# Block sums of the down projection's weights, made in DRAM by accumulating transfers

## The chip, the cores and the metric

The kernel runs on one core of one Trainium2 chip. The metric is the device time of one execution in microseconds (us), of which the runs give a median. The engines are TensorE (PE, with its weight loads as PEld), VectorE (DVE), ScalarE (ACT), GpSimd (POOL) and SyncE (SP, which here only issues transfers). Each runs its own list of instructions in order. Transfers (DMA) are done by 16 DMA engines that all the queues share.

## The reference

Two layers of an encoder over one sequence of 512 tokens and 1024 features. Each layer has a token mixer and a gated feed-forward part; the change touches the last product of the latter.

```python
def mixer_sublayer(x, w_in, pool_w, ...):
    proj = x @ w_in
    ...
    y = bidirectional_ssd(xh, dt_raw, a_log, dt_bias, bm, cm, d_skip)
    ...
    return merged @ w_out

def conv_ffn(x, w_up, ffn_conv_w, ffn_conv_b, w_down):
    h = dwconv_centred(x @ w_up, ffn_conv_w, ffn_conv_b)
    gate, val = jnp.split(h, 2, axis=-1)
    return (jax.nn.gelu(gate, approximate=False) * val) @ w_down

def reference(...):
    for i in range(DEPTH):                       # DEPTH = 2
        x = layer_norm(ALPHA * x + mixer_sublayer(x, ...), ...)
        x = layer_norm(ALPHA * x + conv_ffn(x, ...), ...)
    return x
```

`w_down` of a layer has 2816 rows and 1024 columns.

## The kernel before

**Products.** Every large product is done in fp32 by halves: a tile is split into a rounded high part and the rest, and `mm3` (L381 to L383) makes three matmuls of each product. The weights go through `WeightStream` (L38 to L109): SP issues the load of 1 MB into `wraw` (L66, two buffers), ACT copies the high part `wh` (L90), DVE subtracts it for `wl` (L91), two steps ahead of PE's use.

**Order.** PE's order is the order in which the code is written. On the other engines a scheduler places the instructions by its own estimate of times, within what the data and the buffers allow.

**Mixer.** The state-space mixer of a layer works in eight units `unit(u)` of four heads, two units to a group; they run as background jobs beside the input projection's matmuls. In a unit, ACT's queue brings rows of cumulated decays to all partitions (`m<-acd`), POOL masks them (`affine_select` on `m`, L994), POOL weights the inputs (`xw`, L1051), PE makes states of them (`stp`, L1068), POOL folds the states (`s`, L1076) and adds up the outputs (`y`, L1057 and L1109).

**Down projection.** `strassen_projection` (from L597) does `r @ w_down` with r the gated hidden values, transposed, by Winograd's form of Strassen's scheme. The 22 blocks of 128 rows of `w_down` make 11 pairs; of a pair, b00 and b01 are the left and right half of the even block, b10 and b11 of the odd one. There are seven half-sized products, gathered in the banks v, y, z and x. They want four blocks as they are and four sums of blocks: t1 = b01 - b00, t3 = b11 - b01, t2 = t3 + b00 (up to sign as the code has them) and t4 = b10 - t2. Before the change POOL makes the sums in SBUF as the weights arrive:

```python
g.tensor_tensor(raw[:, 1536:2048], raw[:, 1024:1536], raw[:, 512:1024], op=ALU.subtract)  # L137
g.tensor_tensor(raw[:, 512:1024], raw[:, 512:1024], raw[:, 0:512], op=ALU.subtract)       # L138
self.make_t2(i, raw)            # L126: one more subtraction, into xths or xtls
```

and in the second half `lower` makes t4 (L154). `xths` and `xtls` (L607) are the space of tiles that are free in this stage. For each pair SP loads 512 KB + 256 KB in the first half. The halves of r that don't fit stay in DRAM (`asp`, written by POOL's queue, L1368) and are fetched again by SP (`fetch`, L619; 384 KB per pair), and split by ACT and DVE (`cut`, L621 to L626).

Of the kernel before, what the change touches and what calls it, by code (L numbers as in the profile page):

```python
# [38 lines left out]
class WeightStream:  # L39
# [3 lines left out]
    def __init__(self, nc, tc, pool, plan, ahead, raw_bufs, bufs):  # L43
        self.nc, self.tc, self.pool = nc, tc, pool
        self.plan = plan
        self.subs = [(i, j) for i, r in enumerate(plan) for j in r["order"]]
        self.ahead = ahead
        self.raw_bufs, self.bufs = raw_bufs, bufs
        self.raw = {}
        self.done = {}  # L50
        self.next_raw = 0
        self.next_sub = 0
        self.pos = 0
        self.seq = []
        self.extra = {}
# [4 lines left out]
    def _load(self, i):  # L60
        r = self.plan[i]
        raw = self.pool.tile([P, 2048], F32, tag="wraw", name=f"wraw{i}", bufs=self.raw_bufs)
# [14 lines left out]
    def _split(self, s):  # L77
        i, view = self.seq[s]
        self.load(i + 1)
        src = view(self.raw[i])  # L80
        _, a, b = src.shape
        if s in self.extra:
            pool, bufs = self.extra[s]
        else:
            pool, bufs = self.pool, self.bufs
        h = pool.tile([P, 1024], F32R, tag="wh", name=f"wh{s}", bufs=bufs)
        l = pool.tile([P, 1024], F32R, tag="wl", name=f"wl{s}", bufs=bufs)
# [19 lines left out]
class StrassenWeights:  # L107
# [4 lines left out]
    def __init__(self, nc, tc, pairs):  # L112
        self.nc, self.tc, self.pairs = nc, tc, pairs
        self.t2 = {}
        self.raw0 = None

    def open(self, tiles):

        for t in tiles:
            for i in range(t.shape[1]):  # L120
                self.t2[len(self.t2)] = (t, i)
        self.make_t2(0, self.raw0)

    def make_t2(self, i, raw):
        t, j = self.t2[i]
        self.nc.gpsimd.tensor_tensor(  # L126
            t[:, j, :], raw[:, 1024:1536], raw[:, 512:1024], op=ALU.subtract
        )

    def direct(self, raw):  # L130

        return raw.rearrange("p (a b) -> p a b", a=2)[:, :, 0:512]

    def sums(self, i, raw):

        g = self.nc.gpsimd
        g.tensor_tensor(raw[:, 1536:2048], raw[:, 1024:1536], raw[:, 512:1024], op=ALU.subtract)  # L137
        g.tensor_tensor(raw[:, 512:1024], raw[:, 512:1024], raw[:, 0:512], op=ALU.subtract)  # L138
        if i:
            self.make_t2(i, raw)  # L140
        else:
            self.raw0 = raw
        return raw.rearrange("p (a b) -> p a b", a=2)[:, :, 512:1024]

    def two(self, q):
        t, j = self.t2[2 * q]
        return t[:, j : j + min(2, self.pairs - 2 * q), :]

    def lower(self, q, o, raw):

        t = self.two(q)
        n = t.shape[1]
        b = raw[:, o : o + n * 512].rearrange("p (a b) -> p a b", a=n)
        self.nc.gpsimd.tensor_tensor(t, b, t, op=ALU.subtract)  # L154
        return b

    def plan(self, w, first):

        raws, direct, sums = [], [], []
        for i in range(self.pairs):  # L160
            a, b = 2 * i * P, (2 * i + 1) * P
            raws.append({"srcs": [w[a : a + P, :].unsqueeze(1),
                                  w[b : b + P, 512:1024].unsqueeze(1)], "order": range(2)})
            direct.append((first + i, self.direct))
            sums.append((first + i, partial(self.sums, i)))
        seq = []
        for i in range(self.pairs - 2):
            seq += [direct[i], sums[i]]
        seq += direct[-2:] + sums[-2:]
        odd = w.rearrange("(k two p) c -> two p k c", two=2, p=P)[1, :, :, 0:512]  # L170
        lower, t2, t4 = [], [], []
        for i in range(0, self.pairs, 4):
            n = min(4, self.pairs - i)
            r = first + len(raws)
            raws.append({"srcs": [odd[:, i : i + n, :]], "order": range(n)})
            for k in range(0, n, 2):
                q = (i + k) // 2
                lower.append((r, partial(self.lower, q, k * 512)))
                t2.append((r if q else r - 1, lambda raw, q=q: self.two(q)))
                t4.append((r, lambda raw, q=q: self.two(q)))  # L180
        nq = len(t2)
        for q in range(nq - 2):
            seq += [t2[q], lower[q]]
        return raws, seq + t2[-2:] + lower[-2:] + t4
# [40 lines left out]
def weight_plan(l, w_in, pool_w, w_ssd_proj, w_out, w_up, w_down, down):  # L225
# [71 lines left out]
    r, s = down.plan(w_down[l], len(raws))  # L297
# [4 lines left out]
def tile_hybrid_pool_ssd_convffn_encoder(  # L302
# [60 lines left out]
    downs = [StrassenWeights(nc, tc, KF // 2) for _ in range(NL)]  # L363
# [134 lines left out]
    class Norm:  # L498
# [28 lines left out]
        def add(self, c, c0, ps, first=False, last=False):  # L527
# [3 lines left out]
            if first:  # L531
                nc.vector.scalar_tensor_tensor(xs, xs, ALPHA, ps, op0=ALU.mult, op1=ALU.add)
            else:
                nc.vector.tensor_tensor(xs, xs, ps, op=ALU.add)
# [69 lines left out]
    def strassen_projection(l, name, sw, tags, pool, spill, norm):  # L604
# [7 lines left out]
        sw.open([scratch[0], scratch[1][:, : n - KD, :]])  # L612
        again = scratch[1][:, 3:6, :].rearrange("p a b -> p (a b)").rearrange(
            "p (s a b) -> p s a b", s=2, a=3)
# [3 lines left out]
        def fetch(i):  # L618
            nc.sync.dma_start(again[:, i % 2], spill[i])  # L619

        def cut(i):  # L621
            h = pool.tile([P, 4, 256], F32R, tag=f"ah{i}", name=f"{name}h{i}")
            lo = pool.tile([P, 4, 256], F32R, tag=f"al{i}", name=f"{name}l{i}")
            nc.scalar.copy(h[:, :3], again[:, i % 2])
            nc.vector.tensor_tensor(lo[:, :3], again[:, i % 2], h[:, :3], op=ALU.subtract)
# [20 lines left out]
        for i in range(n - 2):  # L646
# [11 lines left out]
            fetch(i)  # L658
# [14 lines left out]
        for i in (n - 2, n - 1):  # L673
            both(yb, (tags[i], 1), s[i - n + 2], 0, False, i == n - 1)
            both(zb, (tags[i], 2), s[i - n + 2], 1, False, i == n - 1)
            fetch(i)
# [4 lines left out]
        for cc in range(2):  # L681
            norm.add(2 + cc, 512, zb[cc])
            norm.add(2 + cc, 0, zb[cc], True)
# [6 lines left out]
        for q in range(nq - 2):  # L690
# [5 lines left out]
            if q == 0:  # L696
                cut(n - 1)
        t2 = [ws.get(), ws.get()]
# [3 lines left out]
        with tc.high_priority():  # L702
            for cc in range(2):
                norm.add(cc, 512, xb[cc])
                norm.add(2 + cc, 512, xb[cc])
# [62 lines left out]
    for l in range(NL):  # L768
# [483 lines left out]
        for g in range(4):  # L1252
# [16 lines left out]
            ujobs.append(unit(2 * g))  # L1269
            ujobs.append(unit(2 * g + 1))  # L1270
# [70 lines left out]
        for j in range(KF):  # L1341
# [83 lines left out]
```

## Time and profile before

| | before |
|---|---|
| median of 3 runs | 1989.69 us (1988.59 to 1989.8) |
| the profiled execution | 1992.83 us, its span 1991.0 us |
| mean granted TensorE clock | 0.993 |
| PE busy | 1931.9 us, 97% |
| DVE / ACT / POOL busy | 68% / 50% / 31% |
| moved by DMA | 232.19 MB, mean 117 GB/s |

The profile is of one execution, 3.1 us above the median. The span is the time from the first to the last instruction seen. Busy shares are means over the whole; a row of windows gives the same for one stretch. In the rows, `out<-in` are the program's names, and a bracket such as [1.63 <-DVE wl L91] says how long the engine had been idle ahead of the instruction and what ended it.

### The profile page before, as it was taken

The numbers are of one execution on the slowest core, as the hardware profiler recorded it, in microseconds if no ns is written. First come the engines' busy times: TensorE is split into PE (matmuls) and PEld (weight loads), VectorE is DVE, ScalarE is ACT, GpSimd is POOL, SyncE is SP. The second block draws the span as 40 slices with busy tenths as digits, with TensorE's granted clock in tenths as the row PEclk, the third lists the DMA queues.
The fourth block names the chain that finished last, engine by engine and source line by source line (L and its number), as shares of the span: only waits on it lengthen the run. The fifth ranks groups of instructions, "written<-read, shape, count | busy, mean of one in ns | idle before, by whom it ended". The sixth has DMA issues, their size and how long they took to land.

```text
span 1991.0 us, 27368 instructions
## 1 busy us (share of the span) xinstructions
PE 1931.9 (97%) x10449; PEld 1616.0 (81%) x10449; DVE 1348.4 (68%) x1945; ACT 998.4 (50%) x1665; POOL 609.0 (31%) x578
## 2 busy tenths in 40 slices
PE   8999999999999999998999999999999999999997
PEld 7878798988888888876788878989888888888765
DVE  5668576775556656679985685667656566666898
ACT  4767666644333444444457776656443334444443
POOL 1244424241111111168303343242411111111773
PEclk9999999999999999999999999999999999999999
DMA  5444434233241334345225344343332414333541
GB/s 159 123 119 117 127 93 140 86 113 115 76 164 49 121 112 134 106 153 190 83 90 160 106 112 124 110 124 105 85 111 92 168 43 130 121 101 116 180 154 51
DMA packets 174691, 232.19 MB, mean 117 GB/s; under 512 B 7872, under 2 KB 128868, under 8 KB 174560
## 3 DMA queue, kind: packets, MB, share of 16 engines
q1 hardware_dynamic: 152144, 178.80, 28.3%
q10 hardware_dynamic: 17712, 34.08, 7.0%
q0 software_dynamic: 4704, 17.56, 2.5%
q8 instruction: 83, 1.36, 0.3%
q14 instruction: 48, 0.39, 0.1%
HBM read 217.31 MB, written 13.11 MB: 116 GB/s over the span
## 4 chain that ended last, share of the span: by engine, by line
PE 78%; DVE 6%; issue 6%; POOL 4%; DMA 3%; ACT 3%; SPq 0%; POOLq 0%; ACTq 0%; DVEq 0%
PE fg L382 7%; PE fg L381 7%; PE fg L383 7%; PE spp L381 3%; PE zp L381 3%; PE spp L382 3%; PE spp L383 3%; PE zp L382 3%; PE zp L383 3%; PE xp L381 3%; DVE wl L91 3%; PE xp L383 3%; PE xp L382 3%; PE stp L1068 2%; PE ydp L1019 2%
## 5 line engine op out<-in xcount | busy, mean ns | idle before, releaser
L91 DVE TENSOR_TENSOR wl<-wraw,wh 128x1024 fp32r<-128x1024 f32 (+1 forms) x330 | 454.1, 1377 | 251.6 <-ACT wh L90 250.0
L90 ACT CAST wh<-wraw 128x1024 fp32r<-128x1024 f32 (+1 forms) x330 | 341.2, 1035 | 503.6 <-PE fg L382 158.0
L383 PE MATMUL fg<-xthm,wl 128*128 128x512 f32 x640 | 249.0, 389 | 0.0
L381 PE MATMUL fg<-xthm,wh 128*128 128x512 f32 x640 | 249.0, 389 | 0.0
L382 PE MATMUL fg<-xtlm,wh 128*128 128x512 f32 x640 | 249.0, 389 | 0.0
L1001 ACT ACTIVATE m<-m,nac 128x128 f32<-128x128 f32 x512 | 159.6, 392 | 52.2 <-POOL m L994 51.7
L994 POOL TENSOR_SCALAR_AFFINE_SELECT m<-m 128x512 f32<-128x512 f32 x128 | 95.0, 765 | 183.5 <-DMA m<-acd 162.9
L381 PEld LDWEIGHTS fg<-xthm,wh 128*128 128x128 f32 x640 | 120.1, 188 | 25.0
L383 PEld LDWEIGHTS fg<-xthm,wl 128*128 128x128 f32 x640 | 120.1, 188 | 24.9
L382 PEld LDWEIGHTS fg<-xtlm,wh 128*128 128x128 f32 x640 | 120.1, 188 | 24.9
L1109 POOL TENSOR_TENSOR y<-y,yo 128x256 f32<-128x256 f32 x96 | 85.4, 898 | 101.6 <-DVE yo L1101 98.8
L381 PE MATMUL spp<-yth,wh 128*128 128x512 f32 x256 | 110.3, 431 | 0.5 <-ACT yth L1149 0.5
L382 PE MATMUL spp<-ytl,wh 128*128 128x512 f32 x256 | 101.2, 395 | 0.7 <-DVE ytl L1150 0.7
L383 PE MATMUL spp<-yth,wl 128*128 128x512 f32 x256 | 101.1, 395 | 0.0
L479 DVE SCALAR_TENSOR_TENSOR xc<-xp,pcwc,xc 128x510 f32<-128x510 f32 (+1 forms) x128 | 95.2, 745 | 7.2 <-ACT xc L473 5.7
L1002 DVE TENSOR_TENSOR m<-m 128x512 f32<-128x512 f32 x64 | 46.7, 730 | 64.8 <-ACT m L1001 55.5
L1051 POOL TENSOR_TENSOR xw<-xtok,wst 128x768 f32<-128x768 f32 x32 | 51.3, 1621 | 121.9 <-ACT xtok L943 99.0
L1363 POOL TENSOR_TENSOR r<-cvv,cg 128x512 f32<-128x512 f32 x22 | 28.4, 1292 | 175.1 <-issue 130.4
L381 PE MATMUL zp<-wh,xthf 128*128 128x256 f32 x256 | 77.6, 303 | 0.0
L1286 POOL TENSOR_TENSOR g<-g,acc 128x512 f32<-128x512 f32 x16 | 27.5, 1720 | 162.3 <-ACT g L1247 150.3
L381 PE MATMUL zp<-wh,xthi 128*128 128x256 f32 x256 | 77.1, 301 | 0.0
L382 PE MATMUL zp<-wl,xthf 128*128 128x256 f32 x256 | 73.0, 285 | 0.0
(403 smaller groups left out, 5214.0 us busy)
## 6 DMA issues: line engine op xcount, KB each, us to landing
wraw<-in_w_in_dram SPq DMA_DIRECT2D x56, 1024.0 KB, 5.5
wraw<-in_w_up_dram SPq DMA_DIRECT2D x44, 1024.0 KB, 5.2
m<-acd ACTq DMA_DIRECT2D x64, 512.0 KB, 4.9
wraw<-in_w_ssd_proj_dram SPq DMA_DIRECT2D x16, 1024.0 KB, 5.1
wraw<-in_w_down_dram SPq DMA_DIRECT2D x22, 512.0 KB, 3.6
asp<-r POOLq DMA_DIRECT2D x22, 384.0 KB, 2.9
xtls<-asp SPq DMA_DIRECT2D x22, 384.0 KB, 3.8
wraw<-in_w_in_dram SPq DMA_DIRECT2D x16, 512.0 KB, 5.3
```

The source lines that it names most:

```text
L90: self.nc.scalar.copy(hv, src)
L91: self.nc.vector.tensor_tensor(lv, src, hv, op=ALU.subtract)
L381: mm(lhsT=ah, rhs=bh, start=first, stop=False)
L382: mm(lhsT=ah, rhs=bl, start=False, stop=False)
L383: mm(lhsT=al, rhs=bh, start=False, stop=last)
L479: nc.vector.scalar_tensor_tensor(dst[:, o0:o1], ps[:, o0 + s : o1 + s], tap, dst[:, o0:o1], op0=ALU.mult, op1=ALU.add,)
L994: nc.gpsimd.affine_select(out=mv, in_=mv, pattern=[[0, NCH], [1 - 2 * d, P]], compare_op=ALU.is_ge, fill=NEG, base=0, channel_multiplier=2 ...
L1001: nc.scalar.activation(mc, mc, AF.Exp, bias=nac[:, c, col : col + 1])
L1002: nc.vector.tensor_tensor(m[:, 0], m[:, 0], m[:, 1], op=ALU.add)
L1019: nc.tensor.matmul(ps[q * 64 : (q + 1) * 64, c * 64 : (c + 1) * 64], lhsT=m[:, 0, t0 : t0 + 64], rhs=xtok[:, c, hh * 64 : (hh + 1) * 64], ...
L1051: nc.gpsimd.tensor_tensor(h4(xw[:, d]), h4(xtok[:, d : d + 3, :]), hb(wst, d, d + 3, d), op=ALU.mult)
L1109: nc.gpsimd.tensor_tensor(y[:, c, :], y[:, c, :], yo[:, d, :], op=ALU.add)
```

## The change

The sums are no longer made by POOL in SBUF. Each layer has three new tensors in DRAM, `t13` (t1 and t3 side by side), `t2` and `t4`, and eight transfers make them from `w_down`, issued on POOL's queue: four copies, and then four transfers with `accum_op=ALU.add`, which add the source to what stands in the destination. One is issued after each `unit(u)`. Every one moves 11 x 128 x 512 values, 2.88 MB, in 1408 rows of 2 KB. Since all of them add, t1, t3, t2 and t4 are plain sums here, and the signs move to the other operand (`q[:, 1]`, `q[:, 3]`) and to three of the final additions (`norm.add(..., op=ALU.subtract)`).

In the down projection the loads of a pair are now 256 KB + 256 KB of `w_down` and 512 KB of `t13`, later `t2`, `b10` and `t4`. The space of `xths` holds two more raw buffers (`raw_at`) in the first half and two split tiles (`cut_at`) in the second; that of `xtls` holds five buffers for the fetched r in place of two, fetched three pairs ahead.

```diff
@@ WeightStream._load, _split
+        if i in self.raw_at:
+            raw = self.raw_at[i]
...
+        if s in self.cut_at:
+            h, l = self.cut_at[s]
@@ StrassenWeights
-    def make_t2(self, i, raw):
-    def sums(self, i, raw):
-    def lower(self, q, o, raw):
...
+    def __init__(self, nc, dram, l, w, pairs):
+        self.nc, self.pairs = nc, pairs
+        self.t13 = dram.tile([P, pairs, 2, 512], F32, name=f"t13_{l}")
+        self.t2 = dram.tile([P, pairs, 512], F32, name=f"t2_{l}")
+        self.t4 = dram.tile([P, pairs, 512], F32, name=f"t4_{l}")
+        self.blocks = w.rearrange("(k two p) (h c) -> two h p k c", two=2, h=2, p=P)
+        b, t1, t3 = self.blocks, self.t13[:, :, 0, :], self.t13[:, :, 1, :]
+        self.steps = [
+            (t1, b[0, 1]), (t3, b[0, 1]), (self.t2, b[1, 1]), (self.t4, b[1, 0]),
+            (t1, b[0, 0], ALU.add), (t3, b[1, 1], ALU.add),
+            (self.t2, t1, ALU.add), (self.t4, self.t2, ALU.add),
+        ]
+
+    def prepare(self, step):
+        dst, src, *op = self.steps[step]
+        if op:
+            self.nc.gpsimd.dma_start(dst, src, accum_op=op[0], max_dma_last_dim=2048)
+        else:
+            self.nc.gpsimd.dma_start(dst, src)
@@ StrassenWeights.plan
+        for i in range(n):
+            raws.append({"srcs": [b[0, 0, :, i : i + 1, :], b[1, 1, :, i : i + 1, :],
+                                  self.t13[:, i, :, :]], "order": range(2)})
@@ strassen_projection
-            nc.sync.dma_start(again[:, i % 2], spill[i])
+            nc.sync.dma_start(again[:, i % 5], spill[i])
...
-            fetch(i)
+            for j in range(i + 3 if i else 0, min(i + 4, n)):
+                fetch(j)
@@ the mixer's loop over groups
-            ujobs.append(unit(2 * g))
-            ujobs.append(unit(2 * g + 1))
+            for u in (2 * g, 2 * g + 1):
+                ujobs.append(unit(u))
+                downs[l].prepare(u)
@@ the gated hidden values
-            nc.vector.tensor_tensor(q[:, 1], a21, r[:, 1], op=ALU.add)
+            nc.vector.tensor_tensor(q[:, 1], a21, r[:, 1], op=ALU.subtract)
...
-            nc.vector.tensor_tensor(q[:, 3], r[:, 0], r[:, 2], op=ALU.subtract)
+            nc.vector.tensor_tensor(q[:, 3], r[:, 0], r[:, 2], op=ALU.add)
```

PE's order stays the same. POOL's does not, and the scheduler doesn't leave one transfer to a unit: it puts all 16 of them into units 0 and 1 of the first layer. In the rows `m0_3` is the decay tile of head 3 of layer 0 (four heads to a unit, made three heads ahead of their use), `y0_1` and `xw0_1` belong to unit 1 of layer 0, a longer last number only tells tiles apart, and `t13_0`, `t2_0`, `t4_0` are the DRAM tensors of layer 0.

The first place is POOL's order at the start of unit 0 of layer 0. Before:

```order
L785 DMA dsk0_158<-in_d_skip_dram 128x32
L781 DMA dtb1_8530<-in_dt_bias_dram 128x64
L783 DMA nea1_8532<-in_a_log_dram 128x64
L1057 TENSOR_TENSOR y0_0_829<-xtok0_0_424,dsk0_158 128x1024
L994 AFFINE_SELECT m0_0_775<-m0_0_775 128x512 x2
L1051 TENSOR_TENSOR xw0_0_826<-xtok0_0_424,wst0_752 128x768
L994 AFFINE_SELECT m0_1_792<-m0_1_792 128x512 x2
L1051 TENSOR_TENSOR xw0_0_826<-xtok0_0_424,wst0_752 128x768
L1076 TENSOR_TENSOR s0_0_2_921<-s0_0_1_902,tot0_763 128x512
L994 AFFINE_SELECT m0_2_809<-m0_2_809 128x512 x2
L1076 TENSOR_TENSOR s0_0_3_939<-s0_0_2_921,tot0_763 128x512
```

and now (L138 is the accumulating transfer, L140 the copy):

```order
L140 DMA t13_0_83<-in_w_down_dram 1408x1x512 x2
L140 DMA t2_0_84<-in_w_down_dram 1408x1x512
L140 DMA t4_0_85<-in_w_down_dram 1408x1x512
L138 DMA t13_0_83<-in_w_down_dram 1408x1x512 x2
L138 DMA t2_0_84<-t13_0_83 1408x512
L992 AFFINE_SELECT m0_0_782<-m0_0_782 128x512 x2
L992 AFFINE_SELECT m0_1_799<-m0_1_799 128x512 x2
L992 AFFINE_SELECT m0_2_816<-m0_2_816 128x512 x2
L1049 TENSOR_TENSOR xw0_0_833<-xtok0_0_430,wst0_759 128x768 x2
L1055 TENSOR_TENSOR y0_0_836<-xtok0_0_430,dsk0_164 128x1024
L138 DMA t4_0_85<-t2_0_84 1408x512
L1074 TENSOR_TENSOR s0_0_2_928<-s0_0_1_909,tot0_770 128x512
```

Seven transfers of layer 0 now stand ahead of the first mask `m0_0`, and the eighth stands ahead of the state `s0_0_2`. The accumulating ones wait: t1 += for t1's copy, t3 += for t3's copy, t2 += for t1 += and t2's copy, t4 += for t2 +=. The three masks stand together, ahead of both halves of `xw0_0`.

The second place is POOL's order at the end of unit 1 of layer 0, ahead of the first instruction of unit 2 that PE waits for, `xw0_2`. Before:

```order
L994 AFFINE_SELECT m0_8_1377<-m0_8_1377 128x512 x2
L994 AFFINE_SELECT m0_9_1449<-m0_9_1449 128x512 x2
L1109 TENSOR_TENSOR y0_1_1252<-y0_1_1252,yo0_1_1_1596 128x256
L994 AFFINE_SELECT m0_10_1516<-m0_10_1516 128x512 x2
L1109 TENSOR_TENSOR y0_1_1252<-y0_1_1252,yo0_1_1_1596 128x256
L1109 TENSOR_TENSOR y0_1_1252<-y0_1_1252,yo0_1_2_1609 128x256 x2
L1109 TENSOR_TENSOR y0_1_1252<-y0_1_1252,yo0_1_0_1647 128x256
L1109 TENSOR_TENSOR y0_1_1252<-y0_1_1252,yo0_1_3_1664 128x256
L1051 TENSOR_TENSOR xw0_2_1756<-xtok0_2_1142,wst0_752 128x768 x2
```

and now:

```order
L1074 TENSOR_TENSOR s0_1_3_1506<-s0_1_2_1432,tot0_770 128x512
L138 DMA t2_1_87<-t13_1_86 1408x512
L992 AFFINE_SELECT m0_10_1525<-m0_10_1525 128x512 x2
L1107 TENSOR_TENSOR y0_1_1260<-y0_1_1260,yo0_1_1_1605 128x256
L1107 TENSOR_TENSOR y0_1_1260<-y0_1_1260,yo0_1_2_1618 128x256
L1107 TENSOR_TENSOR y0_1_1260<-y0_1_1260,yo0_1_1_1605 128x256
L1107 TENSOR_TENSOR y0_1_1260<-y0_1_1260,yo0_1_2_1618 128x256
L138 DMA t4_1_88<-t2_1_87 1408x512
L1107 TENSOR_TENSOR y0_1_1260<-y0_1_1260,yo0_1_0_1656 128x256
L1107 TENSOR_TENSOR y0_1_1260<-y0_1_1260,yo0_1_3_1673 128x256
L1049 TENSOR_TENSOR xw0_2_1765<-xtok0_2_1150,wst0_759 128x768 x2
```

The last two transfers of layer 1 stand here, each ahead of work of the mixer: t2_1 += waits for t13_1's first accumulation and for t2_1's copy, t4_1 += for t2_1 +=. Layer 1's four copies stand in unit 0, behind `s0_0_2`, and its first two accumulations in unit 1.

## Rows read from the trace of the kernel before

**Rows 1.** The page's first part: busy time, share and instructions of each engine.

```profile
PE 1931.9 (97%) x10449; PEld 1616.0 (81%) x10449; DVE 1348.4 (68%) x1945; ACT 998.4 (50%) x1665; POOL 609.0 (31%) x578
```

**Rows 2.** Windows, down projections: stretch, length, busy PE PEld DVE ACT POOL, PEclk, DMA share, GB/s.

```profile
871.90:941.90 70.00, 62.28 (x251) 47.36 (x250) 65.18 (x41) 31.31 (x34) 61.20 (x36) 0.98 0.61 196
941.90:992.30 50.40, 49.54 (x215) 39.38 (x213) 45.58 (x60) 21.25 (x25) 17.75 (x7) 1.00 0.29 90
1864.00:1934.00 70.00, 62.12 (x256) 46.93 (x255) 67.90 (x42) 32.28 (x35) 57.85 (x31) 1.00 0.61 202
1930.00:1976.00 46.00, 44.91 (x216) 36.28 (x215) 41.65 (x56) 17.96 (x21) 15.57 (x7) 1.00 0.09 32
```

**Rows 3.** Timeline of POOL, one pair: start, duration, engine, line, operation.

```profile
899.43 2.27 POOL L137 TENSOR_TENSOR wraw<-wraw 128x512 f32<-128x512 f32 x1
901.78 1.89 POOL L138 TENSOR_TENSOR wraw<-wraw 128x512 f32<-128x512 f32 x1
903.75 2.16 POOL L126 TENSOR_TENSOR xths<-wraw 128x512 f32<-128x512 f32 x1
```

**Rows 4.** Timeline of DVE, the same stretch.

```profile
902.44 4.55 DVE L91 TENSOR_TENSOR wl<-wraw,wh 128x1024 fp32r<-128x1024 f32 x2
906.92 2.05 DVE L625 TENSOR_TENSOR dp_l<-xtls,dp_h 128x768 fp32r<-128x768 f32 x1
908.89 4.54 DVE L91 TENSOR_TENSOR wl<-wraw,wh 128x1024 fp32r<-128x1024 f32 x2
```

**Rows 5.** One tile's instructions (xths, DVE): count, least/median/greatest ns, first and last start.

```profile
L91 DVE TENSOR_TENSOR wl<-xths,wh x16: 1203/1214/1226, 941.6 to 1964.3; 128x1024 fp32r<-128x1024 f32 x16
```

**Rows 6.** Timeline of PE, end of the first half of layer 0's down projection.

```profile
935.25 0.63 PE L382 MATMUL dp_v<-wl,ah 128*128 128x512 f32 x1
935.67 0.63 PE L383 MATMUL dp_v<-wh,al 128*128 128x512 f32 x1
...
938.03 0.39 PE L383 MATMUL dp_x<-wh,al 128*128 128x512 f32 x1
938.26 0.39 PE L381 MATMUL dp_x<-wh,ah 128*128 128x512 f32 x1
```

**Rows 7.** The page's DMA queues: packets, MB, share of 16 engines' span.

```profile
q1 hardware_dynamic: 152144, 178.80, 28.3%
q10 hardware_dynamic: 17712, 34.08, 7.0%
q0 software_dynamic: 4704, 17.56, 2.5%
```

**Rows 8.** Timeline of POOL, the last of its transfers at the start.

```profile
11.04 0.55 POOL L783 DMA_DIRECT2D nea<-in_a_log_dram  x1 [3.21 <-DMA pcwc<-in_ssd_conv_w_dram]
11.57 0.54 POOL L785 DMA_DIRECT2D dsk<-in_d_skip_dram  x1
```

**Rows 9.** Windows of the stretch in which the new transfers stand, columns as in 2.

```profile
12.00:165.00 153.00, 149.45 (x1038) 132.95 (x1037) 97.02 (x142) 102.56 (x196) 43.49 (x47) 0.99 0.44 120
12.00:71.00 59.00, 59.00 (x402) 53.47 (x401) 36.70 (x59) 30.25 (x41) 3.62 (x4) 1.00 0.41 119
```

**Rows 10.** Timeline of POOL, units 0 and 1 of layer 0.

```profile
71.40 1.22 POOL L994 TENSOR_SCALAR_AFFINE_SELECT m<-m 128x512 f32<-128x512 f32 x2 [0.97 <-DMA m<-acd]
76.81 1.47 POOL L1051 TENSOR_TENSOR xw<-xtok,wst 128x768 f32<-128x768 f32 x1
82.73 1.19 POOL L1076 TENSOR_TENSOR s<-s,tot 128x512 f32<-128x512 f32 x1 [4.45 <-ACT s L1074]
...
157.07 4.79 POOL L1109 TENSOR_TENSOR y<-y,yo 128x256 f32<-128x256 f32 x5
166.13 2.91 POOL L1051 TENSOR_TENSOR xw<-xtok,wst 128x768 f32<-128x768 f32 x2 [4.28 <-ACT xtok L943]
```

**Rows 11.** Timeline of PE, the matmuls that read xw of units 0 and 2.

```profile
78.10 1.02 PE L1068 MATMUL stp<-xw,btok 128*128 128x256 f32 x4
...
169.70 1.03 PE L1068 MATMUL stp<-xw,btok 128*128 128x256 f32 x4
```

**Rows 12.** One tile's instructions (asp), POOL's issues: count, least/median/greatest ns.

```profile
L1368 POOL DMA_DIRECT2D asp<-r x22: 577/582/604, 661.7 to 1864.4; - x22
```

**Rows 13.** Window with the densest transfers of the down projection, columns as in 2.

```profile
890.00:900.00 10.00, 8.26 (x35) 6.11 (x34) 9.94 (x5) 5.57 (x6) 9.11 (x6) 1.00 0.83 291
```

More of the change, by code (lines that the diff above doesn't have):

```diff
@@ L49, in __init__ @@
         self.raw = {}
+        self.raw_at = {}
+        self.cut_at = {}
         self.done = {}
@@ L107 @@
 class StrassenWeights:
[L112 to L122, printed above, removed]
-    def make_t2(self, i, raw):
[L125 to L128, printed above, removed]
@@ L145, in two @@
-    def two(self, q):
-        t, j = self.t2[2 * q]
-        return t[:, j : j + min(2, self.pairs - 2 * q), :]
-    def lower(self, q, o, raw):
[L151 to L157, printed above, removed]
-        raws, direct, sums = [], [], []
[L160 to L165, printed above, removed]
+    def __init__(self, nc, dram, l, w, pairs):
[10 more added lines that the diff above has]
+        ]
@@ new lines, in prepare, with plan, view @@
+    def prepare(self, step):
+        dst, src, *op = self.steps[step]
+        if op:
+            self.nc.gpsimd.dma_start(dst, src, accum_op=op[0], max_dma_last_dim=2048)
+        else:
+            self.nc.gpsimd.dma_start(dst, src)
+    def plan(self, first):
+        n, b = self.pairs, self.blocks
+        self.first = first
+        raws, direct, sums = [], [], []
+        def view(o, n=2):
+            return lambda raw: raw[:, o : o + n * 512].rearrange("p (a b) -> p a b", a=n)
+        for i in range(n):
+            raws.append({"srcs": [b[0, 0, :, i : i + 1, :], b[1, 1, :, i : i + 1, :],
+                                  self.t13[:, i, :, :]], "order": range(2)})
+            direct.append((first + i, view(0)))
+            sums.append((first + i, view(1024)))
@@ L166, in plan @@
         seq = []
-        for i in range(self.pairs - 2):
+        for i in range(n - 2):
             seq += [direct[i], sums[i]]
         seq += direct[-2:] + sums[-2:]
-        odd = w.rearrange("(k two p) c -> two p k c", two=2, p=P)[1, :, :, 0:512]
         lower, t2, t4 = [], [], []
[L172 to L180, printed above, removed]
@@ L181, in plan @@
-        nq = len(t2)
-        for q in range(nq - 2):
+        for i in range(0, n, 2):
+            m = min(2, n - i)
+            t2.append((first + len(raws), view(0, m)))
+            lower.append((first + len(raws), view(m * 512, m)))
+            raws.append({"srcs": [self.t2[:, i : i + m, :], b[1, 0, :, i : i + m, :]],
+                         "order": range(2)})
+        for i in range(0, n, 4):
+            m = min(4, n - i)
+            for k in range(0, m, 2):
+                t4.append((first + len(raws), view(k * 512, min(2, m - k))))
+            raws.append({"srcs": [self.t4[:, i : i + m, :]], "order": range(2)})
@@ L183, in plan @@
+        for q in range(len(t2) - 2):
             seq += [t2[q], lower[q]]
@@ L296, in weight_plan @@
         seq += [a[0], b[0], a[1], b[1]]
-    r, s = down.plan(w_down[l], len(raws))
+    r, s = down.plan(len(raws))
     return raws + r, seq + s
@@ L362, in tile_hybrid_pool_ssd_convffn_encoder @@
     raws, seq = [], []
-    downs = [StrassenWeights(nc, tc, KF // 2) for _ in range(NL)]
+    downs = [
+        StrassenWeights(nc, dram, l, w_down[l], KF // 2) for l in range(NL)
+    ]
     for l in range(NL):
@@ L525, in root, with add @@
             return y
-        def add(self, c, c0, ps, first=False, last=False):
+        def add(self, c, c0, ps, first=False, last=False, op=ALU.add):
             c1 = c0 + ps.shape[1]
@@ L611, in strassen_projection @@
                    for t in ("xth", "xtl")]
-        sw.open([scratch[0], scratch[1][:, : n - KD, :]])
-        again = scratch[1][:, 3:6, :].rearrange("p a b -> p (a b)").rearrange(
-            "p (s a b) -> p s a b", s=2, a=3)
+        more = scratch[0].rearrange("p a b -> p (a b)").rearrange("p (s b) -> p s b", s=2)
+        for i in range(n):
+            if i % 4 > 1:
+                ws.raw_at[sw.first + i] = more[:, i % 2]
+        again = scratch[1].rearrange("p a b -> p (a b)")[:, : 5 * 768].rearrange(
+            "p (s a b) -> p s a b", s=5, a=3)
         second = {}
         def fetch(i):
-            nc.sync.dma_start(again[:, i % 2], spill[i])
+            nc.sync.dma_start(again[:, i % 5], spill[i])
         def cut(i):
@@ L697, in strassen_projection @@
                 cut(n - 1)
+        parts = base.tile([P, 4, 1024], F32R, tag="xth", name=f"xthp{l}")
+        for i in range(2):
+            ws.cut_at[ws.pos + 4 + i] = (parts[:, 2 * i], parts[:, 2 * i + 1])
         t2 = [ws.get(), ws.get()]
```

35 lines of the change are left out of this document (12 added, 23 removed).

## The prediction

> **What bounds the kernel now.** I read four views in this order. First the busy shares [rows 1]: PE works 97% of the span, so only a stage in which PE waits has anything to give. Second the windows of the two down projections [rows 2]: in their first halves PE works 62.28 and 62.12 of 70 us, in the second halves 49.54 of 50.4 and 44.91 of 46, while POOL is busy 61.20 and 57.85 us of the first halves. Idle PE time there is 7.7 + 7.9 + 0.9 + 1.1 = 17.6 us. Third the timelines of that stage: POOL does three subtractions a pair, 2.27 + 1.89 + 2.16 = 6.3 us [rows 3], and DVE, splitting at the same time, comes round every 908.89 - 902.44 = 6.45 us [rows 4]. A split `wl` takes 2.2 us there, and 1.21 us where it reads `xths`, in the halves in which POOL does little [rows 5]. PE itself would need 24 matmuls of 0.23 us a pair, 5.5 us [rows 6]. So a pair goes at POOL's and DVE's pace, about 0.9 us slower than PE's. Fourth, the same matmul comes every 0.42 us at 935 us and every 0.23 us at 938 [rows 6]: after waits PE ran some twelve matmuls at half pace, another 2.3 us.
>
> **What the change removes.** All 33 subtractions of POOL and the t4 sums go from each down projection. DVE is then left with two splits of 1.21 [rows 5] where each took 2.2, and at most 2.05 us of `cut` [rows 4]: 4.5 us a pair, under PE's 5.5. The idle 17.6 us and the 2.3 us are the ceiling of the gain: **20 us**, and I take it whole. Signs and final additions are as many instructions as before: nothing. More is loaded, 1 MB of weights and 384 KB of r a pair, in 5.5 us 261 GB/s; the densest 10 us of the stage moved 291 GB/s at a share of 0.83 [rows 13], so this fits, with two more raw buffers and r fetched three pairs ahead.
>
> **What it adds.** Sixteen transfers of 2.88 MB. Their price is engine time: queue q1 held all 16 engines for 28.3% of 1991 us for 178.80 MB, which is **9.1 us** for 2.88 MB; by q0 it would be 8.2, by q10 11.8 [rows 7]. None of these rows is of a transfer from DRAM to DRAM. I take 9.1 for a copy, because q1 moves most of the same kind of data. No row shows an accumulating transfer. It reads two blocks and writes one. From below it costs what a copy does (8.2); from above three passes (3 x 11.8 = 35.4); I take two passes, **18.2**, since a copy is one read with one write and the second read is what is added.
>
> The Trainium skill, page "Collectives: The Full Stack", section "The bandwidth ceiling: the fold count and why AG ≠ RS ≠ AR", says that a reducing transfer goes at about half a copy's rate because its two source reads share one ring. No run here shows it yet; by it the sum is the one above. The page "DMA: Bandwidth & Descriptors", section "Latency and other measured facts", speaks against the change: it has copies between DRAM tensors at 207 to 214 GB/s, from which I estimate 13.7 us a copy. Doubled for accumulation, that would end at about 2187 us.
>
> POOL's own time for issuing is small: 0.54 us for a transfer of 128 rows at the start [rows 8], 0.58 for `asp` [rows 12]. Sixteen are some 10 us on an engine that is 31% busy.
>
> **Where it is paid.** The costly thing is the order. Since POOL waits for a transfer that it must issue behind another (3.2 us ahead of `nea` [rows 8]), everything behind a waiting transfer on its list waits too. The first place of the order shows seven transfers, three with waits, ahead of the first mask `m0_0`; the second shows t2_1 += and t4_1 += ahead of `xw0_2`. PE has no slack against these. In the trace of before the first mask is made at 71.40, `xw` ends at 78.28, and the first `stp` runs from 78.10, the next matmuls right behind [rows 10, 11]; `xw` of unit 2 starts at 166.13 and PE reads it at 169.70. PE's list is written by hand and can't go on with something else. So whatever holds POOL past **165 us** holds PE.
>
> How long is that? POOL can issue from 12 us on [rows 8]. To pass the last wait, t4_1 += must be issued, so the other 15 transfers must be done: 8 copies and 7 accumulations, 8 x 9.1 + 7 x 18.2 = 200 us of all engines. Besides these, the kernel's own loads of the stretch from 12 to 165 us hold a share of 0.44 of 153 us, 67 us [rows 9]; PE's progress needs them, so they are to be added. A landing costs about 2 us more. POOL is through at 12 + 200 + 67 + 2 = 281 in place of 165: **116 us late**. The first part of it shows at once: the first mask must wait for four copies and an accumulation, 4 x 9.1 + 18.2 = 54.6 us; by 71 us the engines have 59 x 0.59 = 35 us free [rows 9], the other 20 run with PE soon at rest, and the mask comes near 93 in place of 71. All later transfers are smaller than the loads' gaps and cost nothing. Layer 1's mixer has none of its own left, nor does its POOL list wait.
>
> The sum, against the profiled execution: 1992.8 + 116 - 20 = 2089 us. That execution lies 3.1 us above the median, so against the median it is 1989.7 + 96 = **2086 us**. With c for a copy and a for an accumulation, the delay is 8c + 7a - 84; it is this that the cases below fill in. With 8.2 and 16.4 it ends at 2066, with 11.8 and 23.6 at 2145: the own range of the forecast.
>
> **Rivals.**
> - *Accumulation costs no more than a copy.* For it: what counts on an engine may be packets, and these are as many. 15 x 9.1 - 84 = 53 us of delay, 2022 us (2009 with 8.2). Against it: it must read twice.
> - *Accumulation is dearer, three passes.* For it: the destination is read and written in one tensor, and nothing in the trace says that the engines do this at their stride. 8 x 9.1 + 7 x 27.3 - 84 = 180, so 2150; by the highest bounds, 11.8 and 35.4, 2228.
> - *The other side: faster.* If the new queue and the loads overlap on the engines, so that the loads' 67 us are not to be added, 15 transfers fit into 165 - 12 - 2 = 151 us when each takes up to 10.1 us. Copies and accumulations at 9.1 would then hold no one (the first five are done at 12 + 46 + 2 = 60, ahead of 71), and the gain of the down projection is left: 1970 us. For it: the window's share of 0.41 leaves engines free more than half of the time [rows 9]. Against it: accumulation must be as cheap as a copy and the sharing free, both at once. With a = 18.2 and free sharing POOL is 49 us late and it ends at 2019.
> - *It doesn't do what it says.* One transfer to a unit would give each a unit's time and no wait; the order shows that all sixteen stand in units 0 and 1, so I count on that and give it no chance of its own.
> - *The gain is not there.* If the new first halves are bound by loads or by DVE all the same, 20 us are missing: 2106, inside the forecast's own range.
>
> **How the numbers follow.** The forecast has 0.47, the cheap accumulation 0.17, the dear one 0.23, the faster case 0.10, and 0.03 that gain and delay cancel. A measurement of this kernel can tell about 0.2%, 4 us, from no change. Faster is the one case that holds no one up, 0.10; the same 0.03; slower all the others, 0.87. The likeliest time is 2086. For 8 in 10 the range takes in the cheap accumulation down to about 2000 and the dear one up to its upper bound, 2225; left out are the faster case and a delay beyond all bounds.
>
> **What will show it.** In the changed kernel's profile: POOL's waits put down to DMA on t13, t2 and t4, over 100 us in total between 12 and 300 us and none later; the first mask near 93 us and the `xw` of unit 2 near 280; PE idle in the same stretch with POOL (`xw`, `s`, `m`) as its releaser; DMA shares of 0.9 there; in the down projections no L137 or L138 on POOL, `wl` at 1.2 us, pairs every 5.5 us, PE busy 68 of 70 us. The engines' time per queue gives c and a. Wrong would be: no long wait of POOL behind a transfer (then the engines take both queues at once or the sums are cheap); a first mask at 71 with the delay elsewhere; a delay that repeats in layer 1's mixer; or down projections that stay at 6.4 us a pair.

## The result, and the profile after

The changed kernel takes 2073.99 us (median of 4 runs, 2067.07 to 2075.36) against 1989.37 before: **1.0419 times**, 95% interval 1.0395 to 1.0442, or 84.6 us more. Forecast were 2086 us in a range of 2000 to 2225, the likeliest case alone 2066 to 2145. The profiled execution has a span of 2073.6 us, 82.6 more than that of before.

The page of the changed kernel, busy time and queues, answers to [rows 1, 7]:

```profile
PE 1944.7 (94%) x10449; PEld 1630.3 (79%) x10449; DVE 1285.8 (62%) x1945; ACT 998.4 (48%) x1666; POOL 464.9 (22%) x516
...
q1 hardware_dynamic: 158000, 196.10, 29.8%
q0 software_dynamic: 21856, 63.70, 11.7%
```

PE is as busy as before, but in a span that is 83 us longer. The new transfers are in q0, 46.1 MB more than before (16 times 2.88).

POOL's timeline in units 0 and 1 of layer 0, the order of the first and second place, answers to [rows 10]:

```profile
11.63 4.23 POOL L140 DMA_DIRECT2D t<-in_w_down_dram  x4
30.58 1.76 POOL L138 DMA_DIRECT2D t<-in_w_down_dram  x1 [14.71 <-DMA t<-in_w_down_dram]
42.53 1.71 POOL L138 DMA_DIRECT2D t<-in_w_down_dram  x1 [10.19 <-DMA t<-in_w_down_dram]
82.19 1.50 POOL L138 DMA_DIRECT2D t<-t  x1 [37.95 <-DMA t<-in_w_down_dram]
91.40 1.22 POOL L992 TENSOR_SCALAR_AFFINE_SELECT m<-m 128x512 f32<-128x512 f32 x2 [7.70 <-DMA m<-acd]
...
125.01 1.51 POOL L138 DMA_DIRECT2D t<-t  x1 [16.77 <-DMA t<-t]
...
258.06 1.51 POOL L138 DMA_DIRECT2D t<-t  x1 [25.67 <-DMA t<-t]
258.98 2.02 POOL L1107 TENSOR_TENSOR y<-y,yo 128x256 f32<-128x256 f32 x2
260.34 3.50 POOL L1049 TENSOR_TENSOR xw<-xtok,wst 128x768 f32<-128x768 f32 x2
```

The first mask comes at 91.40 in place of 71.40, `xw` of unit 2 at 260.34 in place of 166.13. Who waits for whom from 12 to 275 us, POOL's longest (total us, times, longest):

```profile
POOL t L138 <- DMA t<-in_w_down_dram: 80.8, 4, 38.0
POOL m L992 <- DMA m<-acd: 64.9, 8, 21.0
POOL t L138 <- DMA t<-t: 42.4, 2, 25.7
```

The waits for the new transfers are 123 us, but 65 more are for the `m` broadcasts. The queues from 12 to 262 us (packets, MB, share of the time of the 16 DMA engines) and what loads and broadcasts took there to land (median us):

```profile
q0 software_dynamic: 15946, 43.55, 71.5%
q1 hardware_dynamic: 12977, 12.59, 18.6%
q10 hardware_dynamic: 3072, 5.90, 7.6%
...
wraw<-in_w_in_dram SPq DMA_DIRECT2D x9, 1024.0 KB, 25.2
m<-acd ACTq DMA_DIRECT2D x11, 512.0 KB, 12.4
```

The same loads and broadcasts in the kernel before, from 12 to 165 us:

```profile
wraw<-in_w_in_dram SPq DMA_DIRECT2D x9, 1024.0 KB, 7.2
m<-acd ACTq DMA_DIRECT2D x11, 512.0 KB, 5.4
```

The DMA engines are held 0.98 of the 250 us. The windows of that stretch and of the two down projections, columns as in [rows 2]:

```profile
12.00:262.00 250.00, 168.50 (x1072) 146.23 (x1071) 104.07 (x146) 107.06 (x195) 61.29 (x64) 0.85 0.98 249
975.70:1042.00 66.30, 64.26 (x269) 51.36 (x269) 42.60 (x45) 34.04 (x38) 4.50 (x7) 0.97 0.73 255
...
1958.00:2016.00 58.00, 58.00 (x250) 46.80 (x250) 40.90 (x43) 32.36 (x35) 1.65 (x3) 1.00 0.77 258
```

POOL has next to nothing left to do in the down projections, and PE is busy all of 58 us in layer 1 (62.12 of 70 before [rows 2]).

PE's list is the same in all kernels of this study, so the start of one matmul can be compared between two traces. How much later (us) PE is than in the trace of before, at places given by the time of before; the last column is the difference of the spans:

| run | 205 | 640, FFN 0 | 840 | 1010, layer 1 | 1620, FFN 1 | 1850 | span |
|---|---|---|---|---|---|---|---|
| the change | 103.5 | 103.8 | 103.8 | 96.9 | 94.6 | 94.6 | 82.6 |
| no transfers | -1.1 | -2.6 | -2.6 | -14.6 | -14.8 | -14.8 | -26.9 |
| plain copies | 68.9 | 68.9 | 68.9 | 58.1 | 57.0 | 57.0 | 45.2 |
| early, no wait | 95.1 | 95.0 | 94.9 | 88.1 | 88.0 | 88.0 | 75.9 |
| spread over units | 0.8 | 12.9 | 12.9 | 3.2 | 17.7 | 17.7 | 6.2 |
| spread over FFN | 1.1 | -0.5 | 39.1 | 37.3 | 37.3 | 75.3 | 72.4 |
| pieces, units | 14.2 | 25.5 | 25.4 | 16.2 | 36.7 | 36.7 | 25.7 |
| pieces, FFN | 1.1 | -0.4 | -0.4 | 2.5 | 0.5 | 0.5 | 0.5 |
| pieces, FFN, denser | 1.6 | 1.6 | 4.9 | 2.9 | 2.3 | 11.7 | 6.6 |
| pieces, merge and FFN | 0.7 | -0.8 | -0.8 | -10.7 | -10.9 | -10.9 | -22.5 |

FFN is the feed-forward part. Each row is one execution, and the last column can differ by some us from the medians (no transfers: -26.9 here, -20.0 by the medians). The whole loss of the change is made in the first 205 us of the kernel before, and 21 us of it come back, most of it in the down projections.

### The profile page after: what moved, and what is told of

Same layout as the page of the kernel before. It is cut to its first block, busy times and chain, and to the rows that moved or that the text cites. A ratio compares the mean times of both kernels' runs of the same rounds, so it can differ in the third digit from the quotient of the medians.

```text
span 2073.6 us, 27345 instructions
## 1 busy us (share of the span) xinstructions
PE 1944.7 (94%) x10449; PEld 1630.3 (79%) x10449; DVE 1285.8 (62%) x1945; ACT 998.4 (48%) x1666; POOL 464.9 (22%) x516
## 3 DMA queue, kind: packets, MB, share of 16 engines
q0 software_dynamic: 21856, 63.70, 11.7%
## 4 chain that ended last, share of the span: by engine, by line
PE 73%; DMA 9%; issue 7%; DVE 4%; POOL 2%; ACT 2%; another core or an unknown queue 2%; SPq 0%; ACTq 0%; POOLq 0%; DVEq 0%
PE fg L375 7%; PE fg L373 7%; PE fg L374 7%; PE spp L373 3%; DMA m<-acd 3%; PE spp L374 3%; PE spp L375 3%; PE zp L373 2%; PE zp L374 2%; PE zp L375 2%; PE xp L373 2%; PE stp L1066 2%; PE xp L375 2%; PE xp L374 2%
## 5 line engine op out<-in xcount | busy, mean ns | idle before, releaser
L97 DVE TENSOR_TENSOR wl<-wraw,wh 128x1024 fp32r<-128x1024 f32 (+1 forms) x340 | 421.5, 1242 | 315.9 <-ACT wh L96 314.6
L96 ACT CAST wh<-wraw 128x1024 fp32r<-128x1024 f32 (+1 forms) x340 | 348.6, 1028 | 517.5 <-PE fg L374 162.2
L1066 PE MATMUL stp<-xw,btok 128*128 128x256 f32 x192 | 55.5, 410 | 54.5 <-POOL xw L1049 54.4
L471 DVE SCALAR_TENSOR_TENSOR xc<-xp,pcwc,xc 128x510 f32<-128x510 f32 (+1 forms) x128 | 95.3, 745 | 10.9 <-ACT xc L465 9.4
L555 POOL TENSOR_TENSOR x<-x,lnb 128x512 f32<-128x512 f32 x15 | 21.3, 1419 | 295.4 <-DVE x L551 281.7
L1066 PEld LDWEIGHTS stp<-xw,btok 128*128 128x128 f32 x192 | 36.5, 202 | 63.3 <-POOL xw L1049 58.0
```

The lines of the kernel that those rows point to most:

```text
L471: nc.vector.scalar_tensor_tensor(dst[:, o0:o1], ps[:, o0 + s : o1 + s], tap, dst[:, o0:o1], op0=ALU.mult, op1=ALU.add,)
L1066: nc.tensor.matmul(ps[:, d * 256 : (d + 1) * 256], lhsT=btok[:, c, :], rhs=xw[:, d, c - d, :], start=True, stop=True,)
```

## The experiments

**No transfers.** The block sums are left out, the rest of the change stays.

```diff
-                downs[l].prepare(u)
-                                  self.t13[:, i, :, :]], "order": range(2)})
+                                  self.right[:, i, :, :]], "order": range(2)})
```

> No transfer into DRAM; the down projections load plain blocks of w_down in the same sizes in place of t13, t2 and t4, so the block sums are left out. My theory: all of the loss comes from the sixteen transfers and all of the gain from the down projections, so this ends 20 us below the kernel before, 1966 to 1974 us. Rival: the new first halves are bound by their loads, and the gain seen in the changed kernel's trace is work that only caught up after the long waits: 1980 to 1990.

Measured: 1969.01 us, 0.9899 times before (0.988 to 0.9917). The gain is there as forecast, 20 us, and the whole loss is the sixteen transfers'.

**Plain copies.** Same transfers and waits, nothing added up.

```diff
-            self.nc.gpsimd.dma_start(dst, src, accum_op=op[0], max_dma_last_dim=2048)
+            self.nc.gpsimd.dma_start(dst, src)
```

> The eight accumulating transfers become plain copies of the same sources to the same places, with the same waits; so nothing is added up in DRAM. My theory: what POOL waits for is engine time. In the changed kernel's trace a copy takes 7.8 us of all engines and an accumulation 15.9. With 15 copies POOL gets to xw of unit 2 at 12 + 15 x 7.8 + 66 + 2 = 197 in place of 260 us, 63 us earlier, so the run takes 2005 to 2020 us. Rival: the waits are for the chain of landings (issue, landing, next issue), which is as long with copies: 2060 to 2075.

Measured: 2037.66 us, 1.0236 times (1.0221 to 1.0252), between theory and rival. A third of the loss went, not two thirds. The window from 12 to 235 us:

```profile
12.00:235.00 223.00, 167.70 (x1081) 145.36 (x1080) 111.03 (x147) 108.00 (x200) 58.64 (x66) 0.87 0.88 287
```

The DMA engines are held 0.88 of the time, not 0.98: 27 us of rest, in which, as I read it, transfers, masks and loads wait in turn for each other. Here engine time alone did not give POOL's arrival.

**Early, no wait.** Six copies that nobody waits for, about as much engine time as the sixteen.

```diff
+                if l == 0 and u < 6:
+                    big = dram.tile([P, KF, D], F32, name=f"big{u}")
+                    nc.gpsimd.dma_start(big, w_down[0].rearrange("(k p) c -> p k c", p=P))
```

> As the run without transfers (sums left out), with six copies of the whole w_down of layer 0, 11.5 MB each, to DRAM tensors that nobody reads, issued at the same early places of POOL's list; no instruction waits for them. By 7.8 us per 2.88 MB they take 187 us of all engines, as much as the sixteen transfers of the change. My theory: POOL's in-order waits are what costs, not the traffic; the loads keep most of their share and the run takes 1970 to 2000 us. Rival: the traffic itself starves the weight loads of PE (187 + 66 us of engine time where 153 are there), and the run is as slow as the change, 2050 to 2080.

Measured: 2063.55 us, 1.0372 times (1.0349 to 1.0396). My theory that the waits are the cost, and not the traffic, falls: PE is 95 us late without a single wait of POOL for these copies. POOL's timeline shows what it waited for in their place, and the stretch from 12 to 235 us how long loads and broadcasts took:

```profile
98.38 1.22 POOL L993 TENSOR_SCALAR_AFFINE_SELECT m<-m 128x512 f32<-128x512 f32 x2 [84.08 <-DMA m<-acd]
```

```profile
q0 software_dynamic: 13218, 53.66, 65.9%
q1 hardware_dynamic: 12502, 12.09, 18.8%
...
wraw<-in_w_in_dram SPq DMA_DIRECT2D x9, 1024.0 KB, 27.9
m<-acd ACTq DMA_DIRECT2D x11, 512.0 KB, 14.1
```

The weights of the input projection land in 28 us in place of 7, the masks' rows in 14 in place of 5: the first mask comes at 98 us, later than in the change. So traffic by itself is enough for a loss nearly as large. It is not the change's traffic (packets of 4 KB, copies only, placed differently in time), so how much of the change's own loss its waits make isn't settled by this.

**Spread over units.** The block sums are made as in the change; one transfer stands in each unit of its own layer, behind the unit's last addition to `y`.

```diff
-                downs[l].prepare(u)
...
+            with tc.issue_after(last.ins):
+                downs[l].prepare(u)
```

> The change with its result unaltered; each of the eight transfers of a layer is tied behind the last addition to y of one unit, so that one stands in each unit of its own layer. A unit lasts some 55 us and a transfer 8 to 16 us of engine time, so each has landed long before the next one waits for it. My theory: POOL waits for none of them and the gain stays: 1968 to 1980 us. Rival: sixteen transfers cost their engine time wherever they stand, through later loads and later m broadcasts: 1990 or more.

Measured: 1998.72 us, 1.0044 times (1.0028 to 1.0061): 75 us better than the change, yet 30 worse than without transfers. POOL waits for none of them; against the run without transfers PE loses 15 us in each mixer. The chain of waits at one such place, 335 to 357 us:

```profile
334.76 11.06 DMA m<-acd
...
347.28 9.71 DMA m<-acd
```

An `m` broadcast takes 4.9 us in the trace of before (median). Beside this transfer two took 10 and 11, and the mask, the exponentials and PE behind them had no slack for that: PE falls back 5 us there.

**Spread over the feed-forward part,** where no broadcasts run; each behind the product `r` of a pair.

```diff
+PLACES = (0, 1, 2, 3, 4, 5, 7, 9)
...
+            if i in PLACES:
+                with tc.issue_after(last.ins):
+                    downs[l].prepare(PLACES.index(i))
```

> The change with its result unaltered; the eight transfers of a layer are tied behind the product r of pairs 0, 1, 2, 3, 4, 5, 7 and 9 of its own feed-forward part, some 21 us apart, where no m broadcast runs. Spread over the mixer they cost 14 and 15 us a layer, and the chain there went through late m broadcasts (11 us in place of 4.9). Theory now: traffic costs where PE hangs on a transfer without slack; the up projection's loads come 1 MB per 10.6 us with two buffers, so they can be some us late. Expected 1969 to 1975 us, as without the sums. Rival: the engines' time costs PE wherever it stands: again 14 us a layer, 1995 to 2000.

Measured: 2065.31 us, 1.0375 times (1.036 to 1.0391): a miss, 40 us lost in each feed-forward part. From 640 to 915 us ACT waited for the loads of `w_up` (total us, times, longest):

```profile
ACT wh L97 <- DMA wraw<-in_w_up_dram: 72.5, 9, 15.0
```

PE uses 1 MB per 10.6 us there. Compared matmul by matmul in layer 0, it lost up to 5 us with a copy and 9 to 10 with each of the first three accumulations.

**Small packets** was to test whether an engine serves the queues packet by packet.

```diff
-                    big = dram.tile([P, KF, D], F32, name=f"big{u}")
-                    nc.gpsimd.dma_start(big, w_down[0].rearrange("(k p) c -> p k c", p=P))
+                    big = dram.tile([KF * P * 4, 320], F32, name=f"big{u}")
+                    nc.gpsimd.dma_start(big[:, :256],
+                                        w_down[0].rearrange("r (h c) -> (r h) c", h=4))
```

> As the run with six early copies that nobody waits for (sums left out), but with rows of 1 KB in place of 4 KB, so four times as many packets for the same bytes, all six issued at the start. Theory: an engine takes packets of the queues in turn, so a queue's share goes by its packets: a load packet of 1 KB took 52 ns against 181 to 184 ns of one of the new transfers, which leaves the loads 22 percent (22.7 and 24.1 were seen); at 1 KB against 1 KB they get about half, little less than the 0.44 that they need. The mixer of layer 0 then loses 0 to 35 us in place of 96: 1970 to 2005 us. Rival: only the engines' total time counts, and that does not fall (more packets, at best the same time): 2055 or more.

Measured: 2171.13 us, 1.0908 times (1.0887 to 1.0929). It tests something else. The queue moved as many packets as with the large rows, 4 KB each; this run's page and then POOL's timeline:

```profile
q0 software_dynamic: 21696, 86.77, 12.2%
```

```profile
12.05 3.45 POOL L1272 DMA_DIRECT2D big<-in_w_down_dram  x1
61.50 3.45 POOL L1272 DMA_DIRECT2D big<-in_w_down_dram  x1 [45.99 <-issue]
115.30 3.44 POOL L1272 DMA_DIRECT2D big<-in_w_down_dram  x1 [50.35 <-issue]
```

POOL is held 46 and 50 us ahead of the next transfer with no semaphore named, and its first mask comes at 249 us. Behind transfers of 11264 rows the issuing engine was held; behind those of 2816 rows in the run of early copies it wasn't. That it waits until its queue has room is my guess.

**Spread over units, in halves of 256 columns,** meant to give packets of 1 KB.

```diff
+        for c in (slice(0, 256), slice(256, 512)):
...
+                self.nc.gpsimd.dma_start(dst[:, :, c], src[:, :, c])
```

> The change with its result unaltered, one transfer to a unit as in the run spread over the mixer, each in two halves of 256 columns, so that packets have 1 KB. By the theory of packets in turn the m broadcasts and loads beside them are delayed less (an m landing near 6 in place of up to 14 us), and of the 14 and 15 us a layer at most half is left: 1978 to 1990 us. Rival: total engine time counts alone: 1998 or more.

Measured: 1998.07 us, 1.0039 times (1.0023 to 1.0055), as with 2 KB. By the trace's records of single packets only the accumulations went over to 1 KB; the copies kept packets of 4 KB. So the theory of packets in turn finds no support, but it was tried on the accumulations alone, and the new queue's time rose as well, from 12.7% to 13.9% of the engines' span.

**Pieces in the units.** Each transfer in its 11 pairs, one piece behind each of eleven POOL instructions of a unit.

```diff
+        i = step % self.pairs
+        dst, src = dst[:, i : i + 1], src[:, i : i + 1]
...
+    def drip(self, tc, ins, n=1):
+        with tc.issue_after(ins.ins):
+            for _ in range(n):
+                self.prepare(self.dripped)
+                self.dripped += 1
```

> The change with its result unaltered; each of a layer's eight transfers is cut into its 11 pairs (128 rows of 2 KB, 0.7 us of all engines for a copy and 1.45 for an accumulation), and one such piece is tied behind each of POOL's eleven instructions of a unit of xw, y and s. Theory: what costs is that a burst of 8 to 16 us of engine time stands in front of an m broadcast or a load that has less slack than that; pieces of at most 1.5 us fit into the slack, and the 29 us that the spread transfers cost shrink to 0 to 12: 1969 to 1981 us. Rival: PE loses a part of the engines' time whatever its grain: 1995 to 2002 us.

Measured: 2013.64 us, 1.0118 times (1.0101 to 1.0135), 15 us worse than whole transfers there. In the mixer this grain is not the answer. Two reasons offer themselves: broadcasts without slack meet some piece at any time (6.0 us by the median, 5.6 beside whole transfers), and POOL's list got 80 issues longer in each layer. Neither was tried by itself.

**Pieces in the feed-forward part,** four behind each of two POOL instructions of a pair.

```diff
+                downs[l].drip(tc, nc.gpsimd.tensor_tensor(
+                    a21, cv[:, 256:], cg[:, 256:], op=ALU.mult), 4)
...
+            downs[l].drip(tc, last, 4)
```

> The same pieces, four behind POOL's product a21 and four behind its product r of each pair in the feed-forward part, so about one per 2.6 us, with the result unaltered. There whole transfers cost 40 us a layer, because ACT waited 72 us for loads of w_up. Theory of bursts: a load of 1 MB that takes 5.3 us alone takes some 9 beside an even background of 0.43 of the engines, under the 10.6 us at which PE uses one; 1969 to 1985 us. Rival: 80 us in two layers are lost at any grain, 2050 or more.

Measured: 1993.98 us, 1.0018 times (1.0008 to 1.0028, 9 runs). The windows of layer 0's feed-forward part and of the start of its down projection:

```profile
640.00:872.00 232.00, 232.00 (x1058) 193.52 (x1058) 139.69 (x178) 97.67 (x119) 87.04 (x123) 1.00 0.75 202
872.00:890.00 18.00, 12.83 (x47) 9.43 (x45) 8.69 (x12) 4.02 (x5) 9.89 (x13) 0.89 0.99 252
```

Here is the answer to the 80 us of whole transfers: in pieces the same bytes, but for the last eight pieces, cost PE nothing, 232.00 of 232 us at full clock with the engines held 0.75 of the time. What is left is lost at the start of the down projection, where the last pieces meet loads that nearly fill the engines by themselves. The same 18 us without transfers:

```profile
872.00:890.00 18.00, 18.00 (x80) 14.58 (x79) 11.35 (x14) 9.48 (x10) 4.50 (x7) 1.00 0.97 351
```

**Pieces, denser,** so that they end earlier: six copies in place of four at a place.

```diff
+        if self.dripped < 4 * self.pairs:
+            n = 6
```

> As the pieces in the feed-forward part, with its result unaltered, but six copies in place of four behind each instruction, so that the last piece is issued at pair 9 of 11, some 40 us ahead of the down projection. In the run before this one PE lost nothing in the 232 us of the feed-forward part and 11 and 7 us at 872 to 890 us of each layer, where eight accumulations met the first loads of the down projection, which alone hold the engines for 0.97 of the time. Theory: only that meeting cost; without it the gain of 20 us stays and the run takes 1968 to 1977 us, faster than the kernel before. Rival: the denser copies (0.7 of the engines with the loads) or the accumulations push the loss elsewhere: 1985 to 1995.

Measured: 1996.01 us, 1.0021 times (1.0012 to 1.003, 12 runs from 1988.84 to 1999.34): a miss, just above the rival's range.

```profile
700.00:760.00 60.00, 60.00 (x267) 49.67 (x266) 34.95 (x45) 22.93 (x28) 25.66 (x36) 1.00 0.79 216
760.00:820.00 60.00, 59.15 (x259) 48.04 (x258) 33.85 (x44) 24.59 (x31) 24.62 (x30) 1.00 0.93 204
```

At 0.79 nothing is lost. At 0.93 PE loses 1 us of 60; it is 6 us late at the end of the feed-forward part (1.6 at its start) and 12 soon after the start of the down projection. But the share doesn't decide by itself. In the run before this one the engines were held 0.92 of a longer stretch, and PE lost nothing in it:

```profile
770.00:872.00 102.00, 102.00 (x452) 84.47 (x451) 59.71 (x76) 41.11 (x51) 43.43 (x54) 1.00 0.92 203
```

Why one kernel falls behind and the other doesn't stays open.

**Pieces in the merge and the feed-forward part.** Copies ahead of the feed-forward part, six behind each product of the merge; accumulations three at a place.

```diff
+                downs[l].drip(tc, nc.gpsimd.tensor_tensor(
+                    g1[i], g1[i], acc[:, j, :], op=ALU.mult), 6)
...
-                    a21, cv[:, 256:], cg[:, 256:], op=ALU.mult), 4)
+                    a21, cv[:, 256:], cg[:, 256:], op=ALU.mult), 3)
```

> The pieces again, with the result unaltered: the copies six behind each of POOL's eight products of the merge (ahead of the feed-forward part), the accumulations three behind each point of the feed-forward part, so the last is issued at pair 7 of 11, about 70 us ahead of the down projection. In the run before this one the engines were held 0.93 of the time from 760 to 820 us, the loads of w_up fell behind by 5 us, and those of the down projection met its start late: 13 us lost. Theory: it is free as long as loads and pieces together stay well below full engines (0.66 and 0.79 there cost nothing); accumulations now take 0.41 beside 0.34. Expected 1968 to 1978 us, faster than the kernel before. Rival: any such traffic costs some 12 us a layer wherever it stands: 1990 to 1998.

Measured: **1970.27 us, 0.9892 times before (0.9875 to 0.9908)**, faster than both kernels and within 2 us of the run without any transfer. From 640 to 890 us PE waits for nothing:

```profile
640.00:700.00 60.00, 60.00 (x298) 51.00 (x298) 35.87 (x46) 27.63 (x34) 20.42 (x25) 1.00 0.73 166
700.00:760.00 60.00, 60.00 (x266) 49.73 (x265) 37.00 (x49) 24.29 (x31) 24.19 (x30) 1.00 0.82 192
760.00:820.00 60.00, 60.00 (x266) 49.69 (x266) 38.01 (x48) 25.90 (x32) 18.06 (x22) 1.00 0.75 186
...
872.00:890.00 18.00, 18.00 (x79) 14.57 (x79) 12.68 (x15) 10.19 (x12) 4.50 (x7) 1.00 0.97 347
```

## Why the prediction was right, and where it was not

- **The gain.** Forecast 20 us; the run without transfers has 20.0 by the medians, and in the change PE goes from 103.8 to 82.6 us late, 21. Layer 0 gives less (103.8 to 96.9) than layer 1 (94.6 to 82.6).
- **The price of a transfer.** From 12 to 30 us only copies ran in the new queue, from 85 to 125 only accumulations. The queue's rows of the two stretches:

```profile
q0 software_dynamic: 1015, 3.86, 58.1%
```

```profile
q0 software_dynamic: 2046, 4.12, 57.1%
```

  That is 0.581 x 18 / 3.86 x 2.88 = 7.8 us of all engines for a copy and 0.571 x 40 / 4.12 x 2.88 = 16.0 for an accumulation. I had taken 9.1 and 18.2: both a sixth too high, their ratio right (2.05). The rivals of the cheap and of the dear accumulation fall. By the trace's records of single packets the copies went in packets of 4 KB and only the accumulations in the 1408 rows of 2 KB, so the two differ in packet size too, and the cheap rival was wrong that the packets are as many. Loads in packets of 2 KB in q1 took 96 ns in the same trace (mean), the accumulations' 184, so the size alone doesn't make the factor; that the second read makes it isn't shown. The Trainium skill's page "Collectives: The Full Stack", section "The bandwidth ceiling: the fold count and why AG ≠ RS ≠ AR", tells of about half the rate in the reducing steps of a ring between cores; the ratio in this trace agrees with it. The 13.7 us that I estimated from the Trainium skill's page "DMA: Bandwidth & Descriptors", section "Latency and other measured facts", don't agree with it: 7.8 were measured.
- **The sum.** The own loads took (0.186 + 0.076) x 250 = 66 us, forecast 67. With the measured prices POOL would be through at 12 + 8 x 7.8 + 7 x 16.0 + 66 + 2 = 254; `xw` came at 260, forecast 281. The first mask came at 91.4, forecast 93, and that is luck: POOL was past the transfers ahead of it at 83.7 and then waited 7.7 us for an `m` broadcast, which the forecast didn't have.
- **The term that was mis-sized, and one that was missing.** The dearer prices make 8 x 1.3 + 7 x 2.2 = 26 us too much. Against that POOL came 6 us after the 254 of the sum, and PE, 94 us late at `xw` of unit 2, was 104 late from 205 us on. By the chain of work these 10 us go to the sixteenth transfer, which the sum leaves out: t4_1 +=, issued at 258 us, took 24 us to land. Beside it an `m` broadcast took 13.7 us in place of 4.9; behind its mask and exponentials ACT copies `u`, and PE waited for that. The broadcast, from the chain of 255 to 310 us, and PE's wait from 262 to 305 us:

```profile
267.98 13.69 DMA m<-acd
```

```profile
PE g0p L373 <- ACT u L1190: 9.3, 1, 9.3
```

  The granted clock was 0.83 in that stretch, and 1.00 in the kernel before from 168 to 200 us; its part isn't separated. So the sentence that all later transfers cost nothing failed at the one transfer that was left. Net the forecast was 12 us high: errors of opposite sign, which is luck in part.
- **The step that failed is the cause.** The prediction said that whatever holds POOL holds PE, and that this was the cost. POOL did wait 123 us for the transfers, but the run without such waits was 95 us late at the same place, with loads that took 28 us and broadcasts that took 14. So the waits aren't needed for a loss of this size; what part of it they make in the change itself is open. The number held since the sum counted the time of the engines, which PE's own loads need as much as POOL's waits do. Where the engines rested between, with plain copies, the same sum fell short: expected 2005 to 2020, measured 2038.
- **The faster rival,** free sharing of the engines, fell as well: they were held 0.98 of the time and the loads' time did add. The forecast that nothing more is lost behind these places held: PE's delay stays at 103.5 to 103.8 from 205 to 840 us.

## What to carry to other kernels

Before work is handed to DMA, work out its time of all engines, add that of the loads beside it, and see that the sum stays well below the stretch: here 60 us at 0.82 were free, while of two runs at 0.92 and 0.93 one fell behind at once and the other only in the next stage. Then look at the grain: in the feed-forward part PE paid for bursts of 8 to 16 us of engine time and not for the same bytes in pieces of 0.7 and 1.5 us, while the broadcasts of the mixer had no slack for either. And tie such transfers to a place: the scheduler put these, whose copies depend on nothing, at the start.

## What was not expected of the hardware

An accumulating transfer between DRAM tensors holds the engines 2.05 times as long as a copy (16.0 and 7.8 us for 2.88 MB); by the trace's records of single packets its packets of 2 KB took 184 ns, and a copy's of 4 KB 181. POOL was held 46 us behind one transfer of 11264 rows with no semaphore named. And 21 MB of DRAM to DRAM traffic, 80 of a layer's 88 pieces, ran beside a PE that worked 232 of 232 us.
